# Seven products instead of eight for five of eight k-tile pairs of gate and up, in an fp32 decoder trunk on one core

## The chip, the cores and the metric

The kernel runs on one core of one Trainium2 chip. The metric is the device time of one execution in microseconds (us), shown as the median of several runs. Beside the runs stands one execution that was taken with the hardware profiler: its trace tells when each instruction started, how long it took and what it waited for. The engines are PE (TensorE, matrix products; its weight loads are listed as PEld), DVE (VectorE, element by element), ACT (ScalarE, copies and activation functions), POOL (GpSimd) and SP (SyncE, which issues the transfers here).

## The reference, cut to what matters

Two decoder layers over one sequence of 256 tokens with 2048 features, everything in float32. The change touches the feed-forward part (FFN) of both layers alone:

```python
def swiglu(h, w_gate_up, w_down):            # h: 256 x 2048, D_FF = 5632
    gate, up = jnp.split(h @ w_gate_up, 2, axis=-1)
    return (jax.nn.silu(gate) * up) @ w_down
...
for i in range(DEPTH):                       # DEPTH = 2
    x = x + rmsnorm(mix, post_mix_g[i])      # mix: gated linear attention, then differential attention
    f = swiglu(rmsnorm(x, pre_ffn_g[i]), ffn_w_gate_up[i], ffn_w_down[i])
    x = x + rmsnorm(f, post_ffn_g[i])
```

Each layer's FFN multiplies 256 tokens by a 2048 x 11264 matrix (gate and up side by side) and the result by a 5632 x 2048 matrix (down).

## The kernel before, in words

**Precision.** Every weight and every activation is split in two: `hi` is the value cast to the format that PE multiplies fast, `lo` is what the cast lost. A product is three matmuls: a_hi·w_hi, a_hi·w_lo and a_lo·w_hi (the method `triple`, lines 345 to 347, and `mm_act`, lines 302 to 304). Weights arrive by DMA as tiles `raw` of 128x1024 numbers; for each, ACT writes `hi` (line 238) and DVE then writes `lo` = raw - hi (line 241). Such a pair of hi and lo is called a *slot* below.

**Stream and ring.** `weight_stream` lists all slots in the order of use. `pump` converts ahead of use: five `raw` buffers take the transfers, and the wide `hi` and `lo` (128x1024) lie in rings of `NRING` = 9 buffers, so PE can be at most nine wide slots behind the conversion. A buffer comes free when PE has made its last matmul with it.

**Gate and up together.** D_FF is cut in 11 chunks of 512 columns. For chunk 0, gate and up are two plain products one after the other (`chunk_act`). For chunks 1 to 10 the method `duo_act` makes gate chunk c and up chunk 11 + c at once; this pair is called a *duo* below. It walks over s = 0 to 7, each s two k-tiles of 128 rows (k1, k2). With two token halves and two column chunks this is a 2 x 2 block product. For s in `FAST` = (0, 3, 6) it takes seven products in place of eight, in Winograd's form of Strassen's scheme: the three sums on the activation side are made once per FFN (`build_forms`, `fast_step`), those on the weight side for every duo by `sums`. Such an s is a *fast pair* here and the others are *plain pairs*. Seven PSUM banks collect the products; `early` and `late` in `gated_duo` combine them on DVE (lines 850 and 854) and apply silu on ACT.

- A plain pair takes two wide slots, and each slot feeds four products (12 matmuls).
- A fast pair takes four slots, called a, c, d and b. Its two raw tiles r1 and r2 are converted as `a` (r1), then four additions of 128x512 (line 251) write new values over r1 and r2 and a tile t2 = `sum`; then r1 is converted again as `c`, t2 as the narrow `d` (128x512), and r2 as `b`. The slots feed two, two, one and two products (6, 6, 3 and 6 matmuls). There is one buffer for the narrow hi and one for the narrow lo.

**Groups.** After the duos of a group in `FF_GROUPS`, the gated result is transposed (`split_T`, line 459) and split into `gT`, and the rows of w_down that belong to it are multiplied: four column chunks (c = 0 to 3), each over 2 slots per chunk of the group (12 matmuls a slot). The result goes to f in SBUF, copied by ACT in the first group (line 937), added by DVE afterwards (line 939).

**Order.** The program is written in the order of use, with `defer` and `tick` putting work a number of steps later. Then a scheduler sets the order of each engine's instructions before the run; at run time each engine goes through its own list strictly in that order.

Of the kernel before, what the change touches and what calls it, by code (L numbers as in the profile page):

```python
# [37 lines left out]
FF_GROUPS = ((0, 1), (2, 3, 4), (5, 6, 7), (8, 9, 10))  # L38
FAST = (0, 3, 6)
# [5 lines left out]
def weight_stream():  # L45
# [17 lines left out]
    def ffn(i):  # L63
        for grp in FF_GROUPS:
            for c in grp:
                if c == 0:
                    chunk(f"w_gu{i}", c)
                    chunk(f"w_gu{i}", 11 + c)
                else:
                    duo(f"w_gu{i}", c, 11 + c)  # L70
            for c in range(4):
                chunk(f"w_d{i}", c, 2 * len(grp), 2 * grp[0])
# [60 lines left out]
class Forms:  # L133


    def __init__(self, fast, diff):
        self.f, self.d = fast, diff
        self.plain = [k for k in range(KT) if k // 2 not in FAST]

    def fast(self, i, which):  # L140
        return tuple(self.f[:, i, p, which, :] for p in range(2))

    def diff(self, kt):
        d, i = self.place(kt)
        return tuple(d[:, i, p, :] for p in range(2))

    def place(self, kt):
        i, n = self.plain.index(kt), self.d[0].shape[1]
        return (self.d[0], i) if i < n else (self.d[1], i - n)


class Trunk:
    def __init__(self, ctx, tc, t):
# [19 lines left out]
        self.pool_lo = set()  # L173
        self.cap = 2
# [58 lines left out]
    def split(self, src, pool=False):  # L233
        nc = self.nc
        w = src.shape[-1]
        tag, bufs = ("", NRING) if w == 1024 else ("5", 1)
        hi = self.ring.tile([P, w], F32R, tag="hi" + tag, name=self.uid("hi"), bufs=bufs)
        nc.scalar.copy(hi, src)  # L238
        lo = self.ring.tile([P, w], F32R, tag="lo" + tag, name=self.uid("lo"), bufs=bufs)
        eng = nc.gpsimd if pool else nc.vector  # L240
        eng.tensor_tensor(out=lo, in0=src, in1=hi.bitcast(F32), op=ALU.subtract)  # L241
        return hi, lo

    def sums(self):
# [3 lines left out]
        t2 = self.ring.tile([P, C], F32, tag="sum", name=self.uid("sum"), bufs=1)  # L248
# [91 lines left out]

    def triple(self, ps, a, w, j, first, last):
# [46 lines left out]
    def build_forms(self, aT, fast, diff, temp):  # L388

        nc = self.nc  # L390
        forms = Forms(fast, diff)
# [9 lines left out]
        def fast_step(i):  # L401
# [10 lines left out]
            split(tuple(fast[:, i, p, :, :] for p in range(2)), v)  # L412

        def diff_step(k, n):
            d, at = forms.place(k)
# [5 lines left out]
            split(tuple(d[:, at : at + n, p, :] for p in range(2)), u)  # L421
# [5 lines left out]
        return forms, steps  # L427
# [456 lines left out]
    def ffn(self, fp, hT, rs, gi, wgu, wd, post, after, name, reload, side=None):  # L884
        nc = self.nc
        temp = self.whole(5, [P, 2 * D], f"{name}_temp")
        both = self.whole(4, [P, KT, 2, P], f"{name}_forms", F32R)
        cut = 4 * len(FAST)
        fast = both[:, :cut, :, :].rearrange("p (f w) h t -> p f h w t", w=4)
        more = fp.tile([P, 2 * len(FAST), 2, P], F32R, tag="diff", name=f"{name}_diff")  # L890
        diff = both[:, cut:, :, :], more
        forms, steps = self.build_forms(hT, fast, diff, temp)
        ss = [self.stat(), self.stat()]
        for gidx, grp in enumerate(FF_GROUPS):
            gT = self.pair(gi, f"{name}_gT{gidx}")
            for i, c in enumerate(grp):
# [3 lines left out]
                if c:  # L900
                    sg = self.gated_duo(hT, forms, wgu, c, rs, new_sg)
                    self.defer(4, lambda sg=sg, gT=gT, i=i: [self.split_T(gT, 4 * i, sg[:, b, :], b) for b in range(2)])
# [16 lines left out]
                def gate_T(sg=sg, gT=gT, i=i):  # L919
                    for b in range(2):  # L920
                        self.split_T(gT, 4 * i, sg[:, b, :], b)

                self.defer(3, gate_T)
# [7 lines left out]
            for c in range(4):  # L931
# [15 lines left out]

                skewed = last and c == 3
                self.chunk_act(
# [287 lines left out]
```

## Time and profile before

| | us |
|---|---|
| median of 3 runs | 2229.57 (2229.40 to 2230.09) |
| profiled execution, its time | 2229.63 |
| its span, first to last instruction | 2227.8 |
| PE busy | 2208.3 (99%) |
| DVE busy | 1601.3 (72%) |
| ACT busy | 1165.2 (52%) |

FFN 0 runs from about 397 to 1108 us of the span and FFN 1 from about 1504 to 2218 us. The granted TensorE clock is 0.999 of full speed over the span. A busy figure is the time in which at least one instruction of the engine was under way; matmuls overlap in a pipeline, so that PE's busy share tells little of gaps that are shorter than one matmul (390 ns).

### The profile page before, as it was taken

How to read it: one execution, taken by the hardware profiler on the slowest of the kernel's cores; microseconds unless marked ns; L12 is line 12 of the kernel's file. 1: busy time of each engine (PE TensorE's matmuls, PEld its weight loads, DVE VectorE, ACT ScalarE, POOL GpSimd, SP SyncE). 2: the span in 40 equal slices, each digit the busy share in tenths (PEclk: the TensorE clock that was granted, in tenths of full speed). 3: DMA queues.
4: the chain of work that ended last, by engine and by line, in shares of the span. 5: the costliest groups of instructions: out<-in, count | busy, mean ns of one | idle time of the engine just before them, and what ended most of it. 6: DMA issues, size and time to landing. Idle time of an engine off the chain costs nothing.

```text
span 2227.8 us, 28028 instructions
## 1 busy us (share of the span) xinstructions
PE 2208.3 (99%) x10310; PEld 1835.7 (82%) x10310; DVE 1601.3 (72%) x2093; ACT 1165.2 (52%) x1602; POOL 39.1 (2%) x68
## 2 busy tenths in 40 slices
PE   8999999999999999999999999999999999999998
PEld 7887888888888888888878888888888888888886
DVE  6865554986885886788665567759778868867975
ACT  8654444755554554455465445546555535544552
POOL 2000000000000000000000000000000000000000
PEclk9999999999999999999999999999999999999999
DMA  8565556565565557557665555556655656565573
GB/s 299 166 174 182 173 179 194 197 233 192 199 228 180 173 204 227 177 199 249 196 225 182 185 183 155 192 177 226 218 180 202 213 170 204 194 215 172 197 255 104
DMA packets 123135, 438.37 MB, mean 197 GB/s; under 512 B 13883, under 2 KB 16612, under 8 KB 121460
## 3 DMA queue, kind: packets, MB, share of 16 engines
q1 hardware_dynamic: 121964, 434.99, 59.4%
q8 instruction: 81, 1.33, 0.2%
q10 hardware_dynamic: 1032, 1.57, 0.2%
q14 instruction: 58, 0.48, 0.1%
HBM read 428.11 MB, written 9.97 MB: 197 GB/s over the span
## 4 chain that ended last, share of the span: by engine, by line
PE 97%; DVE 1%; issue 0%; DMA 0%; ACT 0%; POOL 0%; SPq 0%; DVEq 0%; POOLq 0%; ACTq 0%
PE acc L304 15%; PE acc L302 15%; PE acc L303 15%; PE acc L347 12%; PE acc L345 12%; PE acc L346 12%; PE acc L438 8%; PE acc L439 4%; PE tp L459 1%; PE tp L494 1%; PE tp L347 1%; PE tp L345 1%; PE tp L346 1%; PE acc L968 0%; PE acc L1007 0%
## 5 line engine op out<-in xcount | busy, mean ns | idle before, releaser
L241 DVE TENSOR_TENSOR lo<-raw,hi 128x1024 fp32r<-128x1024 f32 x842 | 1011.8, 1221 | 513.6 <-ACT hi L238 510.3
L238 ACT CAST hi<-raw 128x1024 fp32r<-128x1024 f32 x846 | 873.3, 1052 | 821.2 <-PE acc L304 374.3
L346 PE MATMUL acc<-lo,h_ffn 128*128 128x512 f32 x780 | 304.3, 390 | 0.0
L347 PE MATMUL acc<-hi,h_ffn 128*128 128x512 f32 x780 | 304.1, 390 | 0.0
L345 PE MATMUL acc<-hi,h_ffn 128*128 128x512 f32 x780 | 303.9, 390 | 0.0
L302 PE MATMUL acc<-hi,f_ffn_gT 128*128 128x512 f32 x704 | 274.8, 390 | 0.0
L303 PE MATMUL acc<-lo,f_ffn_gT 128*128 128x512 f32 x704 | 274.1, 389 | 0.0
L304 PE MATMUL acc<-hi,f_ffn_gT 128*128 128x512 f32 x704 | 272.1, 389 | 0.0
L347 PEld LDWEIGHTS acc<-hi,h_ffn 128*128 128x128 f32 x780 | 146.5, 188 | 30.4
L345 PEld LDWEIGHTS acc<-hi,h_ffn 128*128 128x128 f32 x780 | 146.5, 188 | 30.4
L346 PEld LDWEIGHTS acc<-lo,h_ffn 128*128 128x128 f32 x780 | 146.5, 188 | 30.2
L302 PEld LDWEIGHTS acc<-hi,f_ffn_gT 128*128 128x128 f32 x704 | 132.2, 188 | 27.7 <-issue 0.6
L304 PEld LDWEIGHTS acc<-hi,f_ffn_gT 128*128 128x128 f32 x704 | 132.2, 188 | 27.4
L303 PEld LDWEIGHTS acc<-lo,f_ffn_gT 128*128 128x128 f32 x704 | 132.2, 188 | 27.1
L302 PE MATMUL acc<-hi,h_mix 128*128 128x512 f32 x256 | 102.2, 401 | 0.0
L347 PE MATMUL acc<-hi,f_ffn_forms 128*128 128x512 f32 x260 | 101.9, 392 | 0.0
L345 PE MATMUL acc<-hi,f_ffn_forms 128*128 128x512 f32 x260 | 101.8, 392 | 0.0
L346 PE MATMUL acc<-lo,f_ffn_forms 128*128 128x512 f32 x260 | 101.2, 389 | 0.0
L303 PE MATMUL acc<-lo,h_mix 128*128 128x512 f32 x256 | 100.8, 394 | 0.0
L304 PE MATMUL acc<-hi,h_mix 128*128 128x512 f32 x256 | 100.5, 393 | 0.0
L438 PE MATMUL acc<-h_mix,hi 128*128 128x512 f32 x272 | 96.7, 400 | 0.0
L438 PE MATMUL acc<-h_q,hi 128*128 128x512 f32 x256 | 92.4, 401 | 0.0
(227 smaller groups left out, 3352.9 us busy)
## 6 DMA issues: line engine op xcount, KB each, us to landing
raw<-in_w_gu_dram SPq DMA_DIRECT2D x352, 512.0 KB, 4.6
raw<-in_w_d_dram SPq DMA_DIRECT2D x176, 512.0 KB, 4.5
raw<-in_gla_w_r_dram SPq DMA_DIRECT2D x32, 512.0 KB, 3.6
raw<-in_gla_w_v_dram SPq DMA_DIRECT2D x32, 512.0 KB, 3.6
raw<-in_gla_w_out_dram SPq DMA_DIRECT2D x32, 512.0 KB, 3.6
raw<-in_w_v_dram SPq DMA_DIRECT2D x32, 512.0 KB, 4.4
raw<-in_w_k_dram SPq DMA_DIRECT2D x32, 512.0 KB, 3.6
raw<-in_diff_w_q_dram SPq DMA_DIRECT2D x32, 512.0 KB, 3.5
```

Source lines behind the costliest of these rows:

```text
L238: nc.scalar.copy(hi, src)
L241: eng.tensor_tensor(out=lo, in0=src, in1=hi.bitcast(F32), op=ALU.subtract)
L302: nc.tensor.matmul(ps, ah, rh, start=(kt == 0), stop=False)
L303: nc.tensor.matmul(ps, ah, rl, start=False, stop=False)
L304: nc.tensor.matmul(ps, al, rh, start=False, stop=(kt == 2 * ns - 1))
L345: nc.tensor.matmul(ps, ah, wh, start=first, stop=False)
L346: nc.tensor.matmul(ps, ah, wl, start=False, stop=False)
L347: nc.tensor.matmul(ps, al, wh, start=False, stop=last)
L438: nc.tensor.matmul(ps, lh, aT.both(kt), start=(kt == 0), stop=False)
L439: nc.tensor.matmul(ps[:, SEQ:], ll, aT.hi(kt), start=False, stop=(kt == KT - 1))
L459: nc.tensor.transpose(tp[:, j, :], src[:, j * P : (j + 1) * P], self.ident)
L494: nc.tensor.transpose(tp[:, j, :], xc[:, j * P : (j + 1) * P], self.ident)
```

## The change

Five things are changed together. `FAST` becomes (0, 2, 3, 5, 6), so that five of the eight pairs of a duo take seven products. The groups become (0, 1), (2, 3), (4, 5), (6, 7), (8, 9, 10). The narrow hi and lo get three buffers each: two in a pool of the FFN, and a third in a place called `room` inside a large tile. For groups of two chunks, the first two of the four column chunks of w_down are made together by the new `two_chunks`: first the two slots of the group's first chunk for column chunk 0, then those for column chunk 1, then the same for the group's second chunk. The tiles of the forms and of gT are laid out anew, since the fast forms take more room and the differences for plain pairs less; gT of a group's third chunk has a tile of its own.

```diff
-FF_GROUPS = ((0, 1), (2, 3, 4), (5, 6, 7), (8, 9, 10))
-FAST = (0, 3, 6)
+FF_GROUPS = ((0, 1), (2, 3), (4, 5), (6, 7), (8, 9, 10))
+FAST = (0, 2, 3, 5, 6)
...
-            for c in range(4):
+            first = 0
+            if len(grp) == 2:
+                first = 2
+                for s in (0, 2):
+                    for c in range(2):
+                        chunk(f"w_d{i}", c, 2, 2 * grp[0] + s)
+            for c in range(first, 4):
                 chunk(f"w_d{i}", c, 2 * len(grp), 2 * grp[0])
...
-    def split(self, src, pool=False):
+    def places(self, w):
+
+        if w == 1024:
+            pool, tag, bufs = self.ring, "", NRING
+        else:
+            pool, tag, bufs = self.fp, "5", 2
+            self.n_narrow += 1
+            if self.n_narrow % 3 == 0:
+                return self.room
+        return [pool.tile([P, w], F32R, tag=n + tag, name=self.uid(n), bufs=bufs) for n in ("hi", "lo")]
+
+    def split(self, src, gp=False):
         nc = self.nc
         w = src.shape[-1]
-        tag, bufs = ("", NRING) if w == 1024 else ("5", 1)
-        hi = self.ring.tile([P, w], F32R, tag="hi" + tag, name=self.uid("hi"), bufs=bufs)
+        hi, lo = self.places(w)
         nc.scalar.copy(hi, src)
...
+    def two_chunks(self, aT, w, s0, evac_of):
+
+        ps = [[self.acc(), self.acc()], None]
+        for half in (0, 2):
+            for c in range(2):
+                if ps[c] is None:
+                    ps[c] = [self.acc(), self.acc()]
+                for s in (half, half + 1):
+                    wp = self.take(w, (c, s0 + s))
+                    for b in range(2):
+                        self.mm_act(ps[c][b], aT, b, s, wp, 4)
+                        if s == 3:
+                            evac_of(c)(b, ps[c][b])
+                        if b:
+                            self.free()
+                        self.tick()
...
-        both = self.whole(4, [P, KT, 2, P], f"{name}_forms", F32R)
-        cut = 4 * len(FAST)
-        fast = both[:, :cut, :, :].rearrange("p (f w) h t -> p f h w t", w=4)
-        more = fp.tile([P, 2 * len(FAST), 2, P], F32R, tag="diff", name=f"{name}_diff")
-        diff = both[:, cut:, :, :], more
-        forms, steps = self.build_forms(hT, fast, diff, temp)
+        self.fp = fp
+        first = self.whole(4, [P, 4, 2, 4, P], f"{name}_fast", F32R)
+        rest = self.whole(2 * gi + 1, [P, KT, 2, P], f"{name}_rest", F32R)
+        n = 4 * (len(FAST) - 4)
+        more = rest[:, :n, :, :].rearrange("p (f w) h t -> p f h w t", w=4)
+        m = n + 2 * (8 - len(FAST))
+        forms = Forms(first, more, rest[:, n:m, :, :])
+        room = rest[:, m : m + 4, :, :].rearrange("p (r w) h t -> p r (w h t)", w=2)
+        self.room = [room[:, i, :] for i in range(2)]
+        steps = self.build_forms(hT, forms, temp)
...
-            gT = self.pair(gi, f"{name}_gT{gidx}")
+            gT = Split([self.whole(2 * gi, [P, KT // 2, 2, SEQ], f"{name}_gT{gidx}", F32R)])
...
+            done = 0
+            if len(grp) == 2:
+                done = 2
+                self.two_chunks(gT, wd, 2 * grp[0], evac_of)
+            for c in range(done, 4):
                 skewed = last and c == 3
```

In the changed kernel the same statements have other line numbers: ACT's hi is line 259, DVE's lo line 261, the additions of `sums` line 271, the three matmuls of a product in a duo lines 382 to 384, the DVE operations of `gated_duo` lines 886 and 890, ACT's copy out of the first bank in `early` line 897 (861 before), the lo of `split_T` line 498, and the addition into f line 983.

**Where the order moves, first place: DVE inside the second duo of a group.** Names carry the buffer's number: `raw` are r1 and r2 of a fast pair, `sum` its t2. Before, the part of a duo from the `a` of one fast pair to the plain slots after it:

```order
L241 TENSOR_TENSOR lo_1205_6499<-raw_1189_6403,hi_1204_6497 128x1024
L251 TENSOR_TENSOR raw_1189_6403<-raw_1189_6403,raw_1192_6415 128x512
L251 TENSOR_TENSOR raw_1192_6415<-raw_1192_6415 128x512
L251 TENSOR_TENSOR sum_1206_6507<-raw_1189_6403,raw_1192_6415 128x512
L251 TENSOR_TENSOR raw_1189_6403<-sum_1206_6507,raw_1189_6403 128x512
L241 TENSOR_TENSOR lo_1211_6526<-sum_1206_6507,hi_1210_6524 128x512
L462 TENSOR_TENSOR f_ffn0_gT2_0_6020<-tp_1194_6430,f_ffn0_gT2_0_6020 128x4x128
L241 TENSOR_TENSOR lo_1208_6514<-raw_1189_6403,hi_1207_6512 128x1024
L241 TENSOR_TENSOR lo_1213_6533<-raw_1192_6415,hi_1212_6531 128x1024
L241 TENSOR_TENSOR lo_1216_6545<-raw_1197_6447,hi_1215_6543 128x1024
L241 TENSOR_TENSOR lo_1219_6563<-raw_1200_6465,hi_1218_6561 128x1024
```

With the change, the second of two fast pairs that now follow each other (s = 2 and 3) in a duo:

```order
L261 TENSOR_TENSOR lo_1248_6637<-raw_1220_6491,hi_1247_6636 128x1024
L261 TENSOR_TENSOR lo_1251_6649<-raw_1225_6525,hi_1250_6648 128x1024
L271 TENSOR_TENSOR raw_1225_6525<-raw_1225_6525,raw_1228_6545 128x512
L271 TENSOR_TENSOR raw_1228_6545<-raw_1228_6545 128x512
L271 TENSOR_TENSOR sum_1252_6655<-raw_1225_6525,raw_1228_6545 128x512
L271 TENSOR_TENSOR raw_1225_6525<-sum_1252_6655,raw_1225_6525 128x512
L261 TENSOR_TENSOR lo_1257_6673<-sum_1252_6655,hi_1256_6672 128x512
L261 TENSOR_TENSOR lo_1254_6661<-raw_1225_6525,hi_1253_6660 128x1024
L261 TENSOR_TENSOR lo_1259_6689<-raw_1228_6545,hi_1258_6688 128x1024
L261 TENSOR_TENSOR lo_1262_6707<-raw_1233_6565,hi_1261_6706 128x1024
```

The first row is the `b` of the pair before, and the narrow lo stands directly behind the additions with the lo of `c` next, with no other work between them. Over the program DVE's list has 982 rows of line 261 (902 of line 241 before), 400 rows of additions (240 before) and 64 additions into f (48 before); PE's list has 1180 rows for each of the lines 382 to 384 (1220 of each of 345 to 347 before).

**Second place: ACT's copy out of the first bank.** It is the first step of `early` and waits until PE has made the product of slot `a` at s = 6. Before, in such a duo:

```order
L238 CAST hi_1229_6628<-raw_1209_6516 128x1024
L238 CAST hi_1232_6640<-raw_1214_6535 128x1024
L861 COPY sg_1241_6667<-acc_1174_6362 128x512
L238 CAST hi_1235_6649<-raw_1217_6547 128x1024
L238 CAST hi_1238_6661<-raw_1220_6565 128x1024
L238 CAST hi_1227_6618<-sum_1223_6595 128x512
```

With the change, in the second duo of the group (6, 7):

```order
L259 CAST hi_1356_7134<-raw_1336_7022 128x1024
L259 CAST hi_1359_7146<-raw_1341_7062 128x1024
L259 CAST hi_1365_7170<-sum_1361_7153 128x512
L897 COPY sg_1397_7300<-acc_1321_6981 128x512
L259 CAST hi_1362_7158<-raw_1341_7062 128x1024
L259 CAST hi_1367_7186<-raw_1344_7080 128x1024
L259 CAST hi_1370_7204<-raw_1347_7092 128x1024
```

Before, the copy stands behind the hi of `b` of s = 6 and of a plain slot of s = 7. Now `hi_1359` is slot `a` of s = 6, and the copy stands ahead of the hi of `c` of the same pair (`hi_1362`), which so comes after it on ACT. The copy stands at this pair in duos 1, 3, 5, 7, 9 and 10 of each layer, ahead of the hi of `c` in all of them; in duos 2, 4, 6 and 8 it stands behind the hi of `a` of the next duo's first pair.

52 lines of the change are left out of this document (29 added, 23 removed).

## The prediction

> **What bounds the kernel now.** I read the page first, then the stretches of FFN 0, the waits there, and the order of time on PE, DVE and ACT inside one group.
>
> ```profile
> PE 2208.3 (99%) x10310; PEld 1835.7 (82%) x10310; DVE 1601.3 (72%) x2093; ACT 1165.2 (52%) x1602; POOL 39.1 (2%) x68
> ...
> PE 97%; DVE 1%; issue 0%; DMA 0%; ACT 0%; POOL 0%; SPq 0%; DVEq 0%; POOLq 0%; ACTq 0%
> ```
>
> PE carries the chain that ended last. It works without gaps in a duo, so its price there is the distance between starts, not the 390 ns of one matmul:
>
> ```profile
> 600.01 0.39 PE L347 MATMUL acc<-hi,h_ffn 128*128 128x512 f32 x1
> ...
> 622.68 0.39 PE L345 MATMUL acc<-hi,h_ffn 128*128 128x512 f32 x1
> ```
>
> They are 100 matmuls apart: 22.67 / 100 = 0.2267 us each. DVE's 72% hides a difference of stages. The first two rows below are the three duos of group (2, 3, 4) and their part of w_down, the third is all of FFN 0 (columns: stretch, length, busy of PE, PEld, DVE, ACT, POOL, clock, DMA share, GB/s):
>
> ```profile
> 545.00:670.00 125.00, 125.00 (x561) 103.50 (x560) 106.39 (x122) 67.79 (x76) 0.00 (x0) 1.00 0.62 210
> 670.00:738.00 68.00, 68.00 (x306) 56.42 (x305) 42.64 (x46) 29.10 (x30) 0.00 (x0) 1.00 0.56 170
> ...
> 397.00:1108.00 711.00, 710.69 (x3190) 587.72 (x3189) 557.93 (x684) 372.91 (x460) 3.85 (x4) 1.00 0.62 206
> ```
>
> In the duos DVE is at 85%, in w_down at 63%, with PE at 100% in both. What keeps DVE from running further ahead is the ring:
>
> ```profile
> ACT hi L238 <- PE acc L304: 102.2, 64, 4.6
> ACT hi L238 <- DVE raw L251: 90.0, 22, 6.0
> ACT hi L238 <- PE acc L347: 72.1, 46, 5.1
> ```
>
> In FFN 0 ACT waits 102.2 us in w_down and 72.1 us in duos for PE to free a buffer. So the conversion is ahead nearly everywhere, and PE decides. The question is whether that is still so when DVE gets more work per matmul.
>
> **What the change takes from PE.** A duo before has 5 plain pairs of 8 products and 3 fast ones of 7: 61 products, 183 matmuls. Now it is 3 x 8 + 5 x 7 = 59, or 177 matmuls. Six fewer in each of 10 duos of 2 layers are 120, and 120 x 0.2267 = **27.2 us**. That is all PE can gain; w_down keeps its matmuls, the transposes theirs.
>
> **What it adds to DVE.** The prices: two groups of the page, then the order of time on DVE, where I take starts to starts.
>
> ```profile
> L241 DVE TENSOR_TENSOR lo<-raw,hi 128x1024 fp32r<-128x1024 f32 x842 | 1011.8, 1221 | 513.6 <-ACT hi L238 510.3
> L238 ACT CAST hi<-raw 128x1024 fp32r<-128x1024 f32 x846 | 873.3, 1052 | 821.2 <-PE acc L304 374.3
> ```
>
> ```profile
> 561.19 0.69 DVE L251 TENSOR_TENSOR raw<-raw,raw 128x512 f32<-128x512 f32 x1
> 561.92 0.69 DVE L251 TENSOR_TENSOR raw<-raw 128x512 f32<-128x512 f32 x1
> 562.53 0.68 DVE L251 TENSOR_TENSOR sum<-raw,raw 128x512 f32<-128x512 f32 x1
> 563.25 0.69 DVE L251 TENSOR_TENSOR raw<-sum,raw 128x512 f32<-128x512 f32 x1
> 565.13 2.36 DVE L241 TENSOR_TENSOR lo<-raw,hi 128x1024 fp32r<-128x1024 f32 x2 [1.19 <-ACT hi L238]
> ...
> 572.26 0.68 DVE L241 TENSOR_TENSOR lo<-sum,hi 128x512 fp32r<-128x512 f32 x1
> 572.87 0.68 DVE L850 TENSOR_TENSOR hs<-tp,hs 128x512 f32<-128x512 f32 x1
> ```
>
> A wide lo costs 2.36 - 1.22 (its own length) = 1.14 us, a narrow operation 572.87 - 572.26 = 0.61. The four additions take 561.19 to 563.94, 2.75 us, and the lo of `c` cannot start before 565.13: DVE idles 1.19, since ACT must first make the hi of the new r1.
>
> ```profile
> 564.05 2.00 ACT L238 CAST hi<-raw 128x1024 fp32r<-128x1024 f32 x2 [4.33 <-DVE raw L251]
> ...
> 596.60 0.62 ACT L238 CAST hi<-sum 128x512 fp32r<-128x512 f32 x1 [4.84 <-PE acc L347]
> ```
>
> In the changed order the narrow lo stands in that gap. Its hi (0.62) can start as soon as `sum` is there (563.25), so it fits ahead of the hi of `c` at 564.05, and about 0.5 us of idle time stays. A fast pair then costs DVE 3 x 1.14 + 0.61 + 2.8 + 0.5 = 7.33 us for 21 matmuls, 4.76 us of PE; a plain pair 2.28 us for 24 matmuls, 5.44 us. Fast pairs are DVE's, plain ones PE's.
>
> ```profile
> L854 DVE SCALAR_TENSOR_TENSOR sg<-hs,rs_ffn,sg 128x512 f32<-128x512 f32 x40 | 29.7, 743 | 0.2
> L861 ACT COPY sg<-acc 128x512 f32<-128x512 f32 x20 | 11.5, 576 | 0.0
> ...
> 500.98 0.87 PE tp L459 x8
> ```
>
> The rows are one of the groups on DVE, one on ACT and a piece of the chain of waits. A duo's other work on DVE (nine operations of `gated_duo`, two lo of the transposed result) stays: 7 x 0.61 + 2 x 0.66 (line 854 is 0.06 longer than the others) + 2 x 0.61 = 6.8 us. So per duo: 5 x 7.33 + 3 x 2.28 + 6.8 = 50.3, less some 0.8 where the order puts other work into the idle gaps (about three of ten pairs): **49.5 us**. PE needs 177 x 0.2267 = 40.1, plus eight transposes (0.87), **41.0 us**. Each duo costs DVE 8.5 us more than PE. The same count for before (19 wide, 3 narrow, 3 x 2.75, 3 x 1.19, 6.8) gives 42.1 against 42.4 on PE, which fits a DVE that just kept the ring full.
>
> **What covers it.** The ring: nine wide slots at the start of a duo are fast, plain, fast and an `a`, 21 + 24 + 21 + 6 = 72 matmuls or 16.3 us; less a hi and a lo, which the buffer freed last still needs, 16.3 - 2.3 = **14.0 us** of lead.
>
> In w_down of a group of two, PE works 16 x 12 x 0.2267 = 43.5 us, DVE 16 x 1.14 + 8 x 0.61 = 23.1, so the lead comes back in full and then stops at nine slots; what DVE idles there is lost.
>
> The rows that price the forms, and then the stalls by group:
>
> ```profile
> L394 DVE TENSOR_TENSOR f_ffn_temp<-h_ffn 128x256 f32<-128x256 f32 x10 | 4.1, 414 | 0.0
> L394 DVE TENSOR_TENSOR f_ffn_temp<-f_ffn_temp 128x128 f32<-128x128 f32 x12 | 3.1, 282 | 0.0
> ...
> L394 DVE TENSOR_TENSOR f_ffn_temp<-h_ffn 128x512 f32<-128x512 f32 x3 | 2.0, 682 | 0.0
> ```
>
> - Group of two. Up to slot `b` of s = 6 of its second duo, where the plain s = 7 has not helped yet, DVE needs 49.5 + (5 x 7.33 + 4 x 1.14 = 41.2) + 6 additions into f (3.7) = 94.4. PE needs 41.0 + 153 x 0.2267 = 75.7. 94.4 - 75.7 - 14.0: PE stands 4.7 us. There are three such groups a layer: 14.
> - Group (8, 9, 10): one duo more, 4.7 + 8.5 = 13.2.
> - Group (0, 1): one duo, whose lead is thinner since DVE builds the forms just before (17.5 us now, 15.8 before, five fast steps of 2.5 us and three differences of 1.65 by these rows). I take 1.5, from bounds 0 and 5.
>
> That is 28.7 us a layer, **57 us** for both. ACT (52% busy) and DMA (0.62 of its share) have room: a fast pair is 3.8 us of ACT against 7.33 of DVE.
>
> **The other edits.** Three narrow buffers take away waits like the 4.84 us at 596.60; with the old single buffer ACT would stand at adjacent fast pairs. They are what lets the 0.5 us above be so small, and are in the sum already. The sixteen more additions into f (0.61 each) lie in w_down and at the duo's first slots, counted above. `two_chunks` keeps 10.9 us (48 matmuls) of work ahead of the first use of a group's second gT, so nothing waits there. ACT's copy out of the first bank, now ahead of the hi of `c`, ties the conversion to PE: from the end of the `a` products the copy (0.58), a hi (1.05) and a lo (1.22) come before `c` is whole, and PE has 0.68 of `d` to do: up to 2.2 us in six duos a layer, 26 us in all. Where the lead is nil anyway, DVE's additions hide the copy, so I count nothing; it bounds the case where the lead is not nil.
>
> **The sum**, against the profiled execution's own 2229.63 (span 2227.8 and 1.8 around it; the median of runs, 2229.57, is the same): 2229.6 - 27.2 + 57 = 2259.4, and I forecast **2259 us**, slower by 1.3%. Bounds. Least: no idle in fast pairs (47.8 a duo) and the full 16.3 of lead; then only the group of three stands, by some 5 us, 10 in both layers: 2212. Most: 1.19 of idle at each fast pair as today, 3.5 us a duo more, 7 in a group of two and 10 in that of three, 31 a layer: 2259 + 62 = 2321.
>
> **Rivals.**
>
> 1. *The ring and the slack of w_down cover it.* For it: ACT's 72.1 us of waiting for PE inside duos show spare lead, and two duos a group mean that the lead is renewed more often. Against: DVE's total. FFN 0 gets 20 more fast pairs, each 2.75 + 0.61 + 1.14 = 4.5 us, 90 in all, and 7 for additions into f and forms: 558 + 97 + 50 x 0.5 of idle = 680 of the 697 us that PE would take, and DVE cannot use 15 to 20 us of the last w_down, where no duo follows. If it holds: the lower bound, about 2212, faster.
> 2. *A tie.* Stalls are half of my count, either since the copy's 2.2 us in twelve duos is all there is or since gaps are better filled: 2229.6 - 27.2 + 26 = 2228.
> 3. *DVE and ACT take turns worse than counted*, with today's 1.19 at each pair, or the raws come late in w_down: 2300 to 2320. Transfers speak against it; one stretch at the start of the program moved far more than the 210 GB/s of a duo:
>
> ```profile
> 12.00:16.00 4.00, 4.00 (x17) 3.22 (x16) 2.51 (x7) 4.00 (x11) 2.24 (x2) 1.00 1.05 404
> ...
> 1112.00:1116.00 4.00, 2.56 (x16) 1.80 (x14) 4.00 (x5) 3.09 (x9) 0.00 (x0) 1.00 1.01 345
> ...
> 2220.00:2224.00 4.00, 0.00 (x0) 0.00 (x0) 3.15 (x6) 0.72 (x2) 0.55 (x1) 0.76 0.18 65
> ```
>
> 4. *Stalls lower the clock.* When PE had been out of work at the end, the clock fell to 0.76 within 4 us (third row). If each of about 10 stalls did that for 4 us at half speed, 2 us each, 20 in all: 2279. Against it: in the second row PE lacks 1.4 of 4 us and the clock stays 1.00, and a late slot here should hold PE 2 to 3 us at a time. The Trainium skill, page "TensorE: Matmul & The Clock Gate", section "HAM oscillation — how this bites in real kernels", puts the limit at gaps of about 3.4 us; these two rows agree with it.
>
> **Chances.** My forecast, 2240 to 2300: 0.59. Rival 1: 0.12. Rival 2: 0.09. Rival 3: 0.15. Rival 4: 0.05. A measurement of this kernel tells 0.2% (4.5 us) from no change. Faster by more than that: rival 1 and a little of rival 2, 0.13; within it: 0.07; slower: 0.80. The range for 8 in 10 is **2216 to 2312**; the likeliest case's own is 2240 to 2300.
>
> **What would show it.** Right: matmuls of the duos' lines 1180 each instead of 1220; in the changed profile PE waits for DVE's lo (or ACT's hi) of a fast pair, most at s = 5 and 6 of the last duo of a group and through duos 9 and 10, some 50 to 60 us in all; DVE is above 90% busy in duos and near 1795 us in all; ACT's waits for PE inside duos shrink to little, those in w_down stay. Wrong: PE still at 100% in duos 9 and 10, or DVE idle there. If DVE idles about 1.2 us behind each set of additions, rival 3; if PE's waits end with the hi behind the copy alone, rival 2; if the clock is below 1.00 in FFN stretches, rival 4.

## The result, and the profile after

| | before | after |
|---|---|---|
| median of four runs, us | 2229.49 (2228.55 to 2230.09) | 2288.51 (2284.51 to 2291.05) |
| ratio, 95% interval | | 1.0263 [1.0246, 1.0281] |
| span of the profiled execution, us | 2227.8 | 2282.8 |
| mean granted TensorE clock | 0.999 | 0.991 |

The change makes the kernel 2.6% slower; forecast were 2259 us and a range of 2216 to 2312. The first two lines of the page of the changed kernel that answer to those shown of before are the busy times and the shares of the chain that ended last:

```profile
PE 2215.6 (97%) x10190; PEld 1818.3 (80%) x10190; DVE 1784.8 (78%) x2357; ACT 1221.9 (54%) x1682; POOL 38.8 (2%) x68
...
PE 79%; DVE 10%; DMA 5%; issue 3%; ACT 3%; POOL 0%; ACTq 0%; SPq 0%; DVEq 0%; POOLq 0%
```

PE has the 120 matmuls less that were counted (10310 to 10190), DVE 183 us more (1601.3 to 1784.8; 1795 was forecast), and the chain that ran over PE alone (97%) now goes through DVE, ACT and the transfers for a fifth of its length. The stretches that were shown of before, for the changed kernel (stretch, length, busy of PE, PEld, DVE, ACT, POOL, clock, DMA share, GB/s); the second row is FFN 0 as a whole, the last two are short pieces of FFN 0 and FFN 1:

```profile
545.00:670.00 125.00, 120.45 (x532) 97.96 (x531) 111.13 (x131) 68.10 (x77) 0.00 (x0) 1.00 0.57 194
397.00:1130.00 733.00, 707.39 (x3115) 573.36 (x3114) 646.70 (x812) 398.83 (x496) 3.30 (x3) 1.00 0.58 199
...
1020.00:1035.00 15.00, 11.21 (x41) 8.81 (x40) 14.96 (x21) 7.38 (x9) 0.00 (x0) 0.77 0.50 180
1725.00:1740.00 15.00, 13.36 (x53) 10.45 (x52) 12.88 (x15) 9.41 (x11) 0.00 (x0) 0.89 0.44 141
```

PE lacks some 25 of FFN 0's 733 us where it lacked nothing before, DVE is busy for 89% of the first stretch (a piece of w_down in it) and all of the third, and in the last two the clock is 0.77 and 0.89. What PE waited for, by its own waits over the whole program (us in total, times, longest):

```profile
PE acc L382 <- ACT hi L259: 20.8, 18, 3.8
PE acc L322 <- ACT f_ffn_gT L497: 11.5, 8, 1.9
...
PE acc L382 <- ACT f_ffn_rest L259: 6.0, 6, 1.2
PE acc L383 <- DVE lo L261: 5.5, 12, 0.9
PE acc L383 <- DVE f_ffn_rest L261: 2.5, 5, 0.9
```

Lines 382 and 383 are the products of the duos, waiting for a hi or a lo (`f_ffn_rest` is the tile that holds the third narrow buffer, and also the forms of s = 6); line 322 is the start of a product of w_down, waiting for gT. This view shows only the time in which no matmul was under way. The distance between the starts of successive matmuls, less the 0.2267 us that it has in an unbroken row, gives the whole loss. Added up over the program: 20.5 us before and 85.2 after. Of the 85.2, 52.1 lie at the products of the duos and 14.4 at w_down. Counted along PE's list, the waits of over 0.1 us in duos all lie at fast pairs: some 22 us at s = 3 and as much at s = 6, the second of two fast pairs that follow each other, and some 8 us at s = 0 of duo 10. By group, from the same starts:

| waits of PE in the duos, us | FFN 0 | FFN 1 | forecast |
|---|---|---|---|
| group (0, 1) | 1.9 | 1.9 | 1.5 |
| group (2, 3) | 4.2 | 4.0 | 4.7 |
| group (4, 5) | 5.2 | 4.2 | 4.7 |
| group (6, 7) | 5.4 | 4.5 | 4.7 |
| group (8, 9, 10) | 11.7 | 10.7 | 13.2 |

In FFN 0 ACT's waits show the same from the other side. Before, ACT waited 72.1 us inside duos for PE to free a buffer. Now no hi in a duo waits for PE; the hi of `sum` wait for DVE's additions instead, 172 us, and the waits for PE in w_down (line 324) fall from 102.2 us to 42.0:

```profile
ACT hi L259 <- DVE sum L271: 116.8, 28, 6.5
ACT f_ffn_rest L259 <- DVE sum L271: 55.4, 13, 6.5
...
ACT hi L259 <- PE acc L324: 42.0, 22, 7.2
```

The account: the span grew by 55.0 us and 27.2 of matmuls are gone, so 82.2 us were lost. More waits of PE: 85.2 - 20.5 = 64.7. The rest is 17.5. The records of the clock have eight stretches at 0.50 ahead of the last one, with which the program ends: six of 3.41 us and two of 6.83, 34.1 us. PE was busy for 30.8 of them and began 74 matmuls, so half clock cost some 15 (30.8 / 2) to 17 us (74 x 0.2267), nearly all of the rest. One of the eight, at 1141.4 us, lies behind FFN 0, where the kernel with four fast pairs (below) has one too.

### The profile page after: what moved, and what is told of

The parts are those of the page before. It is cut to its first block, busy times and chain, and to the rows that moved or that the text cites. A ratio compares the mean times of both kernels' runs of the same rounds, so it can differ in the third digit from the quotient of the medians.

```text
span 2282.8 us, 28182 instructions
## 1 busy us (share of the span) xinstructions
PE 2215.6 (97%) x10190; PEld 1818.3 (80%) x10190; DVE 1784.8 (78%) x2357; ACT 1221.9 (54%) x1682; POOL 38.8 (2%) x68
## 4 chain that ended last, share of the span: by engine, by line
PE 79%; DVE 10%; DMA 5%; issue 3%; ACT 3%; POOL 0%; ACTq 0%; SPq 0%; DVEq 0%; POOLq 0%
PE acc L322 12%; PE acc L324 12%; PE acc L323 12%; PE acc L382 8%; PE acc L383 8%; PE acc L384 8%; PE acc L474 8%; DVE lo L261 6%; PE acc L475 4%; DMA raw<-in_w_d_dram 4%; ACT hi L259 2%; DVE raw L271 1%; PE tp L382 1%; DVE hs L886 1%; PE tp L495 1%
## 5 line engine op out<-in xcount | busy, mean ns | idle before, releaser
L261 DVE TENSOR_TENSOR lo<-raw,hi 128x1024 fp32r<-128x1024 f32 x882 | 1049.0, 1222 | 348.7 <-ACT hi L259 347.1
L259 ACT CAST hi<-raw 128x1024 fp32r<-128x1024 f32 x886 | 898.9, 1050 | 471.9 <-PE acc L324 252.1
L383 PE MATMUL acc<-lo,h_ffn 128*128 128x512 f32 x660 | 257.8, 391 | 0.0
L384 PE MATMUL acc<-hi,h_ffn 128*128 128x512 f32 x660 | 257.1, 390 | 0.0
L322 PE MATMUL acc<-hi,f_ffn_gT 128*128 128x512 f32 x640 | 244.8, 392 | 11.5 <-ACT f_ffn_gT L497 11.5
L323 PE MATMUL acc<-lo,f_ffn_gT 128*128 128x512 f32 x640 | 250.6, 392 | 0.6 <-DVE lo L261 0.6
L382 PE MATMUL acc<-hi,h_ffn 128*128 128x512 f32 x660 | 244.8, 393 | 0.0
L324 PE MATMUL acc<-hi,f_ffn_gT 128*128 128x512 f32 x640 | 243.3, 390 | 0.0
L259 ACT CAST hi<-sum 128x512 fp32r<-128x512 f32 x67 | 41.7, 622 | 233.4 <-DVE sum L271 233.4
L382 PEld LDWEIGHTS acc<-hi,h_ffn 128*128 128x128 f32 x660 | 124.8, 189 | 27.9 <-ACT hi L259 2.6
L384 PEld LDWEIGHTS acc<-hi,h_ffn 128*128 128x128 f32 x660 | 124.5, 189 | 26.2
L382 PE MATMUL acc<-hi,f_ffn_fast 128*128 128x512 f32 x213 | 87.8, 412 | 14.5 <-ACT hi L259 14.5
L474 PE MATMUL acc<-h_kv,hi 128*128 128x512 f32 x256 | 90.6, 399 | 0.0
```

What stands on the lines that cost most here:

```text
L322: nc.tensor.matmul(ps, ah, rh, start=(kt == 0), stop=False)
L323: nc.tensor.matmul(ps, ah, rl, start=False, stop=False)
L324: nc.tensor.matmul(ps, al, rh, start=False, stop=(kt == 2 * ns - 1))
L382: nc.tensor.matmul(ps, ah, wh, start=first, stop=False)
L383: nc.tensor.matmul(ps, ah, wl, start=False, stop=False)
L384: nc.tensor.matmul(ps, al, wh, start=False, stop=last)
```

## The experiments

The theories at the start: **A**, in a duo with five fast pairs DVE's conversion is slower than PE, and the lead of nine slots does not cover it; **B**, the order of ACT's list (the copy out of the first bank and gT's casts ahead of a hi) makes the hi late; **C**, the clock falls by itself or at gaps shorter than weighed in the prediction.

### DVE without three of the four additions

```diff
-        add(r1[:, :C], r1[:, :C], r2[:, :C])
-        add(r2[:, :C], r2[:, :C], r2[:, C:])
         add(t2, r1[:, :C], r2[:, C:])
-        add(r1[:, C:], t2, r1[:, C:])
```

> Three of the four additions of each fast pair are left out (one stays, so that the narrow tile is written), so the weight-side sums are not computed; PE, ACT and the transfers keep all their instructions. Theory A (DVE's conversion is slower than PE in a duo, and the ring only delays it): DVE needs 5 x (3 x 1.14 + 0.61 + 0.61) + 3 x 2.28 + 6.8 = 36.8 us a duo against 41.0 on PE, so PE's waits inside duos vanish and with them the stretches at half clock; 2202 to 2216 us (the upper end if the waits at the start of w_down, 14 us, stay). Theory B (the order of ACT's list: its copy out of the first bank and its casts of gT wait for PE and hold the conversion up): ACT's list keeps both, so at least half of the 52 us of waits in duos stay: above 2228. Theory C (the clock falls for a reason of its own): seven stretches at half clock stay, with or without waits.

Measured: 2202.09 us, 0.9877 [0.9857, 0.9897] of before. Its page:

```profile
PE 2180.7 (99%) x10190; PEld 1812.9 (82%) x10190; DVE 1589.7 (72%) x2057; ACT 1239.9 (56%) x1682; POOL 39.3 (2%) x68
...
PE 97%; DVE 1%; issue 1%; DMA 0%; ACT 0%; POOL 0%; SPq 0%; DVEq 0%; POOLq 0%; ACTq 0%
```

With 195 us less on DVE everything that was lost is back: PE carries 97% of the chain, its waits sum to 20.7 us as before, there is no stretch of half clock ahead of its end, and the time is 27.4 us under before, which is the 27.2 of the count. So DVE's additions are the cause, as in theory A. Theory B is not excluded by this run alone, since ACT's list was made anew as well: in the changed kernel 16 of the 40 casts of gT stand directly ahead of the hi of a `sum`, in this one 2. Against a large part for B speaks the changed kernel's own trace. In its duos 9 and 10, where most is lost, DVE is busy for 83.9 of 89 us; 4.2 of the rest are its waits for the hi behind its additions:

```profile
975.00:1064.00 89.00, 80.62 (x341) 63.39 (x341) 83.89 (x103) 47.61 (x57) 0.00 (x0) 0.96 0.52 178
...
DVE lo L261 <- ACT hi L259: 4.2, 9, 0.6
```

One more term was not varied by any run: ACT's waits for the transfers of w_down rise from 12.5 to 37.3 us in FFN 0, and what they cost is open.

### Four fast pairs, three fast pairs, and five in half of the duos

```diff
-FAST = (0, 2, 3, 5, 6)
+FAST = (0, 2, 4, 6)
```

> Four fast pairs (0, 2, 4, 6), none next to another, in place of five; groups, buffers and all else as in the change. PE saves 60 matmuls, 13.6 us. Theory A: DVE needs 4 x 7.33 + 4 x 2.28 + 6.8 - 0.6 = 44.6 us a duo against 41.7 on PE, 3 us a duo in place of 8.5; the lead of 14 us covers 6 to 9 us, so waits in duos are below 10 us in all and the clock stays full; with 0 to 14 us of waits at the start of w_down 2216 to 2236 us, some 2222. Theory B: the copy and the casts of gT stand in ACT's list as before, and waits in duos go down in proportion to the fast pairs at most: 2255 or more.

Measured: 2216.91 us (2216.41 to 2217.92), 0.9945 [0.9928, 0.9961] of before: faster than both kernels. PE's waits are 18.9 us; the only stretch of half clock before the end is 3.41 us at 1110.3, behind FFN 0.

```diff
-FAST = (0, 2, 3, 5, 6)
+FAST = (0, 3, 6)
```

> The change with three fast pairs (0, 3, 6) as before, but its groups of two, its joint chunks and its three narrow buffers: what the layout brings without the additional fast pairs. Theory A (only DVE's work per duo decides; PE waits where DVE takes longer than PE): 19 wide and 3 narrow lo and 3 sums are 42 us of DVE against 42.4 of PE, so PE waits no more than before: its waits stay near 20 us, no half-clock stretch inside the FFNs, 2225 to 2233 us (before 2229.6; the sixteen more additions into f, 10 us, are off the path). Rival: the new groups cost by themselves (gT comes late, the lead is used up at each start of w_down, as the 14 us of waits there in the changed kernel suggest): 2236 to 2250.

Measured: 2229.18 us, ratio 1.0000 [0.9990, 1.0009], PE's waits 20.3 us. The groups of two, the joint chunks, the three narrow buffers and the additional additions into f bring and cost nothing by themselves. The pages of the kernels with three and with four:

```profile
PE 2207.9 (99%) x10310; PEld 1835.5 (82%) x10310; DVE 1616.7 (73%) x2109; ACT 1168.9 (52%) x1602; POOL 39.7 (2%) x68
```

```profile
PE 2195.6 (99%) x10250; PEld 1824.3 (82%) x10250; DVE 1699.9 (77%) x2233; ACT 1200.9 (54%) x1642; POOL 38.7 (2%) x68
```

Three, four and five fast pairs: DVE 1616.7, 1699.9 and 1784.8 us, PE's waits 20.3, 18.9 and 85.2. The step from three to four costs DVE 83 us and PE nothing, that from four to five 85 and 66 us: PE waits from a point between on. By the prediction's prices a duo with four costs DVE 49.5 - 7.33 + 2.28 = 44.5 us against 41.0 + 0.7 on PE: 2.8 too much, and two duos of that are within the lead of 14.0.

```diff
-FAST = (0, 2, 3, 5, 6)
+FAST = (0, 2, 4, 6)
+MORE = (0, 2, 4, 6, 5)
+WIDE = (2, 4, 6, 8)
...
-            if s in FAST:
+            if s in FAST or (s in MORE and n1 in WIDE):
```

> Four fast pairs (0, 2, 4, 6) in all duos, and pair 5 too in the first duo of groups (2, 3), (4, 5), (6, 7) and (8, 9, 10). Theory A: the lead of nine slots is full when a group starts; a duo of five uses 8.5 us of 14, a duo of four some 3.5, so a group of two fits (12.0 of 14.0) and PE gains 8 x 0.68 = 5.4 us over four everywhere (2216.9): 2211.5, range 2209 to 2216, PE's waits 19 to 23 us as with four. Rival: the lead is thinner than counted (it was about 10 us at the first fast pair in the changed kernel), then PE waits at the end of the second duo and the clock is halved after it: 2217 to 2232.

Measured: 2225.82 us, 0.9987 [0.9978, 0.9996] of before: the rival. PE's waits are 32.0 us, 13.1 more than with four. They are not where the rival had them: 3.3 us lie at fast pairs, most of them in duo 10, and 10.0 at w_down. The order of time at such a place on DVE, PE and ACT (PE's two rows are the transposes and the first product that uses them; their lines are shifted by 3 in this kernel):

```profile
1731.55 0.75 DVE L893 SCALAR_TENSOR_TENSOR sg<-hs,rs_ffn,sg 128x512 f32<-128x512 f32 x1
```

```profile
1736.72 1.03 PE L498 MATMUL tp<-ident,sg 128*128 128x128 f32 x8
1738.50 0.50 PE L324 MATMUL acc<-hi,f_ffn_gT 128*128 128x512 f32 x1 [0.75 <-ACT f_ffn_gT L500]
```

```profile
1736.92 1.05 ACT L261 CAST hi<-raw 128x1024 fp32r<-128x1024 f32 x1 [1.67 <-PE acc L326]
1737.87 1.07 ACT L500 CAST f_ffn_gT<-tp 128x512 fp32r<-128x512 f32 x2
```

PE makes the eight transposes directly ahead of the products that use them, and ACT has a hi of w_down in its list ahead of the cast of gT, so PE stands 0.75 us. The lists were made before the run; DVE had the gated result ready at 1732.3 (1731.55 + 0.75), so at run time the transposes could have come earlier. Eight such places, 0.8 to 2.1 us each, give 8.8 of the 10.0. In the kernel with four they sum to 1.6 us. So the lead does hold for a duo of five and one of four, as A counted, and what was gained (5.4 us) is lost by the waits at the start of w_down. That the order of the lists causes them is read from this trace; no run changed that order alone.

### The joint chunks of w_down

```diff
-            if len(grp) == 2:
+            if len(grp) == 20:
```

(in the stream and in `ffn`; no group has 20, so four column chunks are made one after the other)

> As the change, without the joint first column chunks: w_down of a group of two runs its four column chunks one after the other, so that the group's second gT is needed after 24 matmuls (5.4 us) and not after 48 (10.9 us). If the waits at the start of w_down (14 us) are the time from the last duo's end to gT of its second chunk, they grow by up to 5.4 us in each of eight groups, 43 us, and the clock falls at more places: 2315 to 2350 us. If they come from something else (ACT standing at a late transfer at a fixed place of its list), they stay: 2280 to 2295.

Measured: 2289.06 us, 1.0267 [1.0240, 1.0293]; the changed kernel has 1.0263. The two runs are 10 us apart (2284.00 and 2294.13); the slower one is the profiled one, and has 13 stretches of half clock where the changed kernel's has eight. Waits for gT at w_down are 18.5 us (14.4 with the joint chunks). What `two_chunks` was to cover is not covered by it, since the transposes and the use stand next to each other in PE's list either way.

### One narrow buffer

```diff
-            pool, tag, bufs = self.fp, "5", 2
-            self.n_narrow += 1
-            if self.n_narrow % 3 == 0:
-                return self.room
+            pool, tag, bufs = self.fp, "5", 1
```

> The change with one buffer for the narrow hi and lo in place of three. The prediction counted 0.5 us of idle time on DVE per fast pair, and said that the buffers keep it that small. Theory A: with one buffer the narrow hi of the next pair has to wait for PE to free the last, which is felt at adjacent pairs (2 and 3, 5 and 6) at least: two per duo of 0.7 us or more, 1.4 to 3.5 us per duo, 28 to 70 us in twenty duos, of which the standing part is most: 2305 to 2345 us. Rival: the narrow part was never what ACT waits for, as the lead is near nil and PE has freed it long before: 2284 to 2294, like the changed kernel.

Measured: 2309.01 us, 1.0359 [1.0340, 1.0378], 20.5 us over the changed kernel. PE's waits rise from 85.2 to 107.6; at the forms of s = 0 to 5 there are 66 waits in place of 32 (36.8 us against 29.7). The expected range is met at its lower end. The two added buffers are worth 20 us with five fast pairs. With three, the kernel with three buffers is as fast as that of before with one; with four it was not tried.

### The lo of slot `b` on GpSimd

```diff
-            self.subs[n] = self.split(self.pending["cbd".index(kind)])
+            self.subs[n] = self.split(self.pending["cbd".index(kind)], kind == "b")
```

> As the change, with the lo of slot b of every fast pair made by POOL in place of DVE (100 of 128x1024; POOL took 2.42 us for such a lo at the program's start, DVE 1.22). Theory A: DVE is relieved of 5 x 1.14 = 5.7 us a duo, 43.8 us against 41.0 on PE, so waits in duos fall from 52 to below 15 us and most stretches at half clock vanish: 2212 to 2232 us, unless DVE's own operations get slower while POOL works. Theory B: waits stay, 2270 or more. If POOL and DVE hold each other up, DVE's lo takes visibly longer than 1.22 us and the gain is lost: 2270 to 2330.

Measured: 2323.26 us, 1.0420 [1.0404, 1.0435]: slower still. The groups of the wide lo, on DVE and on POOL, and one place in order of time (DVE, then POOL):

```profile
L261 DVE TENSOR_TENSOR lo<-raw,hi 128x1024 fp32r<-128x1024 f32 x782 | 1070.0, 1384 | 410.4 <-ACT hi L259 406.0 <-PE acc L323 2.0
```

```profile
L261 POOL TENSOR_TENSOR lo<-raw,hi 128x1024 fp32r<-128x1024 f32 x104 | 262.1, 2520 | 1099.8 <-ACT hi L259 1099.8
```

```profile
697.75 1.23 DVE L261 TENSOR_TENSOR lo<-raw,hi 128x1024 fp32r<-128x1024 f32 x1 [0.55 <-ACT hi L259]
699.64 2.67 DVE L261 TENSOR_TENSOR lo<-raw,hi 128x1024 fp32r<-128x1024 f32 x1 [0.67 <-ACT hi L259]
```

```profile
698.74 2.49 POOL L261 TENSOR_TENSOR lo<-raw,hi 128x1024 fp32r<-128x1024 f32 x1 [8.38 <-ACT hi L259]
```

A lo takes POOL 2.5 us, and a lo on DVE beside it 2.67 instead of 1.22: POOL's ends at 701.23, and DVE's at 702.31, 1.08 later, as if it had only begun then. DVE's mean goes from 1222 to 1384 ns; (1.384 - 1.222) x 782 = 127 us over 100 moved operations, 1.27 us each, more than the 1.14 that a lo costs DVE. So moving these lo to POOL gains nothing. The Trainium skill, page "SBUF — State Buffer", section "SBUF: two separate sides", says that a DVE operation with two inputs in SBUF and a GpSimd operation that reads SBUF lock each other out for the whole instruction; the 2.67 agrees with it.

PE's waits are 135 us in this kernel, nearly all of them below 1.6 us, and only two stretches ran at half clock. That was the reason for the next runs.

### At which gap the clock falls

A first attempt put a transpose of TensorE behind a chain of ACT copies (L983) in w_down:

```diff
+                    for i in range(k + 1):
+                        nc.scalar.copy(x, x if i else fc)
+                    def probe():
+                        nc.tensor.transpose(self.tp()[:, 0, :], x[:, :P], self.ident)
+                    self.defer(2, probe)
```

> Four fast pairs everywhere (2216.9 us), and at 20 places in w_down, where the lead is full, one transpose of TensorE that waits for k + 1 copies on ACT, k from 0 to 9, each size twice, so PE stands once there for some 0.4 + 0.58 k us, from 0.4 to 5.6 (its result is not used). It measures at which length of a single gap the granted clock falls. If the half clock of the changed kernel follows a gap of 3.4 us or more alone: half-clock stretches after the 8 or so longest gaps (k from 6) and none below; some 60 us of gaps and 8 x 1.7 us of half clock, 2280 to 2295 us. If shorter gaps do it (theory C: what counts is the work in a window of 3.41 us, and 2 us of gap in it is enough): stretches from k = 3 or 4 on, 10 to 14 of them, 2285 to 2305 us. If single gaps do nothing and it needs several: no stretch, 2270 to 2280.

Measured: 2218.70 us, one run: no gap came up. The order that is set before the run moved each transpose behind other products until its data were there; PE's waits are 19.5 us. The run shows something else: 110 copies of 0.62 us, 68 us of ACT in w_down, come with only 1.8 us more time. ACT has room there.

In the second attempt every product that follows depends on the chain:

```diff
+                if not last and c > 1:
+                    n = 4 * (1 - gi) + gidx
+                    part = gT.part(0, 8, slice(112, 144), 0)
+                    for i in range(n + 1 if c == 2 else 8 - n):
+                        nc.scalar.copy(part, part.bitcast(F32))
```

> Four fast pairs everywhere (2216.9 us), and at 16 places in w_down (ahead of column chunks 2 and 3 of the first four groups of each layer), where the lead is full, TensorE must stand once: ACT rewrites a piece of gT's hi in place k times, k from 1 to 8, each size twice, and every product that follows reads it. Single gaps of some 1.0 to 5.0 us (0.6 + 0.4 k, and a hi of 1.05 that ACT's list may have between), 45 to 55 us in all. If the half clock of the changed kernel needs a single gap of 3.4 us (the rule the prediction weighed): stretches of half clock after the longest 4 to 8 gaps and after none below 3.4 us: 2270 to 2290 us. Theory C (2 us of missing work within a stretch of 3.41 us is enough): stretches from gaps of some 2 us on, 9 to 13 of them: 2280 to 2300 us. If neither: no stretch, 2262 to 2272 us.

Measured: 2288.06 us, one run; clock 0.987. Now PE stands at each place, up to 4.14 us. Ten of the sixteen gaps were followed by half clock, five of them for 6.83 us, where only four were longer than 3.4 us: theory C. Gaps of 1.52 us and less were followed by none; one of 1.96 was, and one of 2.25 was not:

```profile
651.12 0.50 PE L322 MATMUL acc<-hi,f_ffn_gT 128*128 128x512 f32 x1 [1.52 <-ACT f_ffn_gT L1005]
...
787.69 0.50 PE L322 MATMUL acc<-hi,f_ffn_gT 128*128 128x512 f32 x1 [1.96 <-ACT f_ffn_gT L1005]
...
1669.35 0.50 PE L322 MATMUL acc<-hi,f_ffn_gT 128*128 128x512 f32 x1 [2.25 <-ACT f_ffn_gT L1005]
```

So the length of a gap is not all. The starts of the half-clock stretches tell more. They are 528.76, 665.29, 788.17, 805.24, 924.71 and so on, and every distance between two of them is a whole multiple of 3.413 us (665.29 - 528.76 = 136.53 = 40 x 3.4133; 788.17 - 665.29 = 122.88 = 36 x 3.4133). In the changed kernel all eight lie on such a grid as well. If the program is cut at this grid, one looks at the window ahead. Pairs of windows, the second row of a pair following the first (busy of PE is the first number behind the length; the clock is the third last):

```profile
784.76:788.17 3.41, 1.45 (x7) 0.91 (x6) 3.41 (x5) 2.63 (x5) 0.00 (x0) 1.00 0.73 169
788.17:791.59 3.42, 3.42 (x10) 2.64 (x9) 3.32 (x6) 0.03 (x1) 0.00 (x0) 0.50 0.76 285
...
1665.40:1668.81 3.41, 1.69 (x8) 1.08 (x6) 1.31 (x2) 2.78 (x6) 0.00 (x0) 1.00 0.74 235
1668.81:1672.23 3.42, 2.88 (x13) 2.39 (x14) 0.56 (x1) 0.45 (x2) 0.00 (x0) 1.00 0.57 157
```

The gap of 1.96 lies in one window, which has 1.45 us of work of 3.41; the next window runs at half clock. The gap of 2.25 is cut by the edge at 1668.81: the two windows have 1.69 and 2.88 us of work, and the clock stays.

```diff
+                    def hook(s, b, k=k):
+                        if (s, b) not in ((0, -1), (0, 0)):
+                            return
+                        part = gT.part(0, 8, slice(112, 144), 0)
+                        for i in range(k):
+                            nc.scalar.copy(part, part.bitcast(F32))
```

(two shorter chains at each of the same places, the second after six matmuls)

> The same 16 places, with two shorter gaps each, one ahead of the column chunk and one after its first six matmuls (1.36 us), k copies on ACT each, k from 1 to 4: pairs of gaps of some 1.0 to 2.2 us (to 3.2 with a hi between), 40 to 60 us in all. The rule of a single gap of 3.4 us: no stretch of half clock at all, 2257 to 2277 us. Theory C: a pair within 3.41 us counts together, so stretches at most of the 16 places where the two sum to 2 us or more, 8 to 14 of them, 1.7 us each: 2275 to 2300 us.

Measured: 2278.84 us, one run. Neither: four of the sixteen places have half clock, so the rule of a single gap of 3.4 us fails again, and so does C as it was put (8 to 14). At each of the four the longer gap (1.96 to 2.78 us) lies with 1.9 us or more in one window. Pairs of some 1.5 and 0.8, or 1.8 and 1.6 us, did nothing, since no window had enough of them:

```profile
526.63:530.04 3.41, 1.66 (x6) 1.05 (x6) 1.22 (x1) 1.78 (x5) 0.00 (x0) 1.00 0.75 284
530.04:533.46 3.42, 2.05 (x9) 1.71 (x10) 0.00 (x0) 1.58 (x5) 0.00 (x0) 1.00 0.73 277
...
2048.98:2052.39 3.41, 1.50 (x6) 1.05 (x6) 3.37 (x5) 1.80 (x4) 0.00 (x0) 1.00 0.78 258
2052.39:2055.81 3.42, 1.81 (x5) 1.34 (x5) 3.21 (x5) 2.24 (x5) 0.00 (x0) 0.50 0.45 153
```

In the first pair of rows PE stands 2.25 and 1.62 us within 5.5, and nothing happens; neither window lacks more than 1.75.

## Why the prediction was right, and where it was not

**The direction and its reason: right.** PE's gain is the 27.2 us of the count; without the additions the kernel is 27.4 faster. Behind it DVE is slower than PE in a duo. The step of the fast pair was put at 7.33 us, with 0.5 of idle time. In the changed kernel the additions of two neighbouring fast pairs begin at 1001.36 and 1008.81, 7.45 us apart, with 0.52 of idle time. The order of time on DVE:

```profile
1001.36 0.69 DVE L271 TENSOR_TENSOR raw<-raw,raw 128x512 f32<-128x512 f32 x1
...
1004.07 0.69 DVE L261 TENSOR_TENSOR lo<-sum,hi 128x512 fp32r<-128x512 f32 x1
1005.28 3.50 DVE L261 TENSOR_TENSOR lo<-raw,hi 128x1024 fp32r<-128x1024 f32 x3 [0.52 <-ACT hi L259]
1008.81 0.69 DVE L271 TENSOR_TENSOR raw<-raw,raw 128x512 f32<-128x512 f32 x1
```

The narrow lo stands in the gap, as the prediction read from the order. Over all 100 fast pairs DVE idles 0.64 us on average.

**The waits in the duos: right, the size in part by luck.** 52.1 us against 57, and by group 4.0 to 5.4 against 4.7, 1.9 against 1.5, and 11.7 and 10.7 against 13.2, in the last duo of each group and in duos 9 and 10. The places were put at s = 5 and 6; they are s = 3 and 6, and s = 0 of duo 10. The sum for a group of two has two slips that nearly cancel. PE's 153 matmuls include the six that need slot `b` itself, and a late slot is felt earlier, at `c` of s = 6, after 138. And the lead was taken as PE's time for nine slots, 16.3 us, where DVE is ahead by its own work for them, 2 x 7.33 + 2.28 + 1.14 = 18.1. With both put right, the same prices give 49.5 + 40.1 + 3.7 - 41.0 - 31.3 - 15.8 = 5.2 us at `c` of s = 6, of which 3.2 are there at `c` of s = 3 already. That fits the size and both places.

**The clock: mis-sized.** The likeliest case put it at nothing, and rival 4, with 20 us, had a chance of 0.05. It cost some 15 to 17, and rival 4's sign, a clock below 1.00 in the FFNs, was there. The step that failed is the limit: the prediction held a late slot of 2 to 3 us against a limit of some 3.4 and concluded that the clock stays. The row of before that was taken for support, 1.4 us lacking in a stretch of 4 and a clock of 1.00, agreed with a limit anywhere above 1.4. Two windows of the changed kernel in FFN 1, each with the one behind it: the first holds two waits at s = 3 (1.19 and 0.91 us without a matmul), the second one at the start of w_down (1.95):

```profile
1858.16:1861.57 3.41, 1.31 (x7) 0.73 (x6) 2.91 (x5) 1.85 (x3) 0.00 (x0) 1.00 0.20 78
1861.57:1864.98 3.41, 3.41 (x9) 2.55 (x9) 3.08 (x3) 3.41 (x5) 0.00 (x0) 0.50 0.21 30
1905.94:1909.35 3.41, 1.46 (x8) 1.08 (x7) 3.03 (x4) 2.32 (x4) 0.00 (x0) 1.00 0.99 374
1909.35:1912.77 3.42, 3.42 (x10) 2.68 (x9) 0.62 (x2) 0.00 (x0) 0.00 (x0) 0.50 0.92 297
```

Two waits of about 1 us in one window were enough. The Trainium skill, page "TensorE: Matmul & The Clock Gate", has the window right: section "Part 1: The HAM clock gate (the "warmup" mystery)" says that it is 3413 ns and runs on freely, and the starts of the stretches lie on a grid of 3.413 us. Its rule of gaps of about 3.4 us in the section that the prediction cited does not hold here.

**The start of w_down: mis-sized.** "Nothing waits there" was said, and 14.4 us are lost there. The 10.9 us of `two_chunks` were counted from the program as it is written; in PE's list the transposes stand directly ahead of their use, so the cover does not lie behind them. One place of the changed kernel:

```profile
1771.88 1.03 PE L495 MATMUL tp<-ident,sg 128*128 128x128 f32 x8
1773.90 0.50 PE L322 MATMUL acc<-hi,f_ffn_gT 128*128 128x512 f32 x1 [0.99 <-ACT f_ffn_gT L497]
```

That order fits the joint chunks having made no difference. Why the list is made this way with five fast pairs and hardly with four was not tried.

**ACT's copy at nothing: right; gT's cast: not seen.** The copy out of the first bank waits 53.2 us in all, and costs no more than DVE's additions beside it. A cast of gT, of the result of the duo before, stands ahead of a hi of `sum` at s = 3 of a group's second duo, and waits for PE's transposes:

```profile
594.41 0.59 ACT L497 CAST f_ffn_gT<-tp 128x512 fp32r<-128x512 f32 x1 [4.66 <-PE tp L495]
594.89 0.62 ACT L259 CAST hi<-sum 128x512 fp32r<-128x512 f32 x1
```

PE then stands 1.19 us for that hi, and so in all eight such duos (3, 5, 7 and 9 of both layers). What it is worth by itself was not measured: it lies within the 52.1. An estimate from DVE, which paces these duos: it idles 0.86 to 1.63 us at the additions of s = 3 there, in place of the 0.61 at most others, which is 3.6 us over the eight.

**Rivals.** 1 and 2 are out: the ring covers four fast pairs and not five. 3 is out in its place, since DVE idles 0.52 us behind the additions and not 1.19; that its figure (2300 to 2320) lies nearer than the forecast is chance. In sum, against the profiled executions' own times: 2229.6 - 27.2 + 64.7 of waits (57 forecast) + 17.5 (0 forecast) = 2284.6, and the changed kernel's is 2284.5. The 17.5 is what the account leaves over, so that the sum must close; 15 to 17 of it were counted as half clock. The forecast was 25 us too low for this execution, which its range of 2240 to 2300 was wide enough to hold.

## What to carry to other kernels

Trading matmuls for vector work pays as long as the vector engine, with the lead that the ring gives, keeps up per stage: here four fast pairs took some 12.6 us off the kernel and a fifth cost 71.6 (2288.5 - 2216.9), since each fast pair costs DVE 5.05 us more than a plain one (7.33 - 2.28, the prediction's prices) and saves PE 0.68. Once PE stands at all, count its gaps twice: a gap costs its own length, and the half clock that follows when work is missing for about half of a window. Read what covers a wait from the engine's list, not from the source: work that is written between a producer and its use need not stand there.

## What the runs showed of the hardware

**The clock is granted by windows of 3.413 us.** Over the nine profiled executions that have half-clock stretches ahead of their end, cut at their grids, there are some 5860 windows at full clock. None of those that lacked less than 1.36 us of PE's busy time was followed by a window at half clock; of those that lacked 1.36 to 1.84, 9 of 42 were, and of those that lacked 1.85 or more, all 42. One window of the kernel with three fast pairs, just ahead of its end, lacked 1.91 and was not. So about half a window without matmuls is what counts, not one gap of a length, and the grid lies differently against the program in each execution: a gap of 2.25 us that an edge divided left the clock as it was in two places, and one of 1.96 brought a window at half clock, up to half of 3.41 us more. The blurred zone may come from the ends of matmuls, which are modelled, and from records that are missing; it is not settled. Two gaps of 1.19 and 0.91 us in one window were enough, so that it is their sum that counts.

**POOL and DVE hold each other up.** A subtraction of 128x1024 on POOL took 2.5 us, twice DVE's 1.22, and a DVE subtraction beside it 2.67; 100 such operations cost DVE 127 us.
